# A mixture-of-experts trunk: the first expert position goes from 128 slots and split weights to 64 slots in two column tiles and whole weights

## The chip, the cores and the metric

One NeuronCore of a Trainium2 chip runs the whole program. The metric is the device time of one execution in microseconds, the median of several runs.

## The reference, cut to what matters

A two-layer trunk over 272 tokens (16 meta tokens are dropped at the end) of width 1024, in float32. Each layer has a recurrence, a convolution and an output projection; layer 0 then has a dense SwiGLU, and layer 1 a mixture of eight experts of which each token takes two:

```python
D_MODEL, SEQ, N_EXPERTS, TOP_K, D_FF_EXPERT = 1024, 256, 8, 2, 3584

def moe_swiglu(x, w_router, w_gate, w_up, w_down):
    t = x.reshape(B * L, D)
    logits = (t @ w_router).astype(jnp.float32)
    top_val, top_idx = lax.top_k(logits, TOP_K)
    top_w = jax.nn.softmax(top_val, axis=-1)
    gates = jnp.sum(jax.nn.one_hot(top_idx, N_EXPERTS) * top_w[..., None], axis=1)
    out = jnp.zeros_like(t)
    for e in range(N_EXPERTS):
        out = out + gates[:, e:e + 1] * swiglu(t, w_gate[e], w_up[e], w_down[e])
    return out.reshape(B, L, D)          # swiglu: (silu(x @ w_gate) * (x @ w_up)) @ w_down
```

On the inputs used, the 256 kept tokens fall on the experts 0 to 7 as 179, 20, 32, 107, 98, 10, 2 and 64 (each token counts twice).

## The kernel before

All weights pass once through the core, in pieces of 128 x 1024 float32 (512 KB each, a few of 256 KB). Pieces 0 to 243 (`DENSE`) belong to the two mixers and the dense layer, the last of them to `w_hg_out` (8 pieces) and `w_out` (8). The 672 pieces behind them are the eight experts, 84 for each: 28 gate, 28 up, 28 down. SyncE (SP) issues every load, in one order, from one queue.

The experts are worked off by **position**. Position 0 is always expert 7 (`FIRST`), so that its loads need not wait for the routing; positions 1 to 7 are the other experts by falling number of tokens. The order is 0, 2, 3, 4, 5, 6, 7 (`ORDER`), and the pieces of position 1 (`SIDE`) are strewn among those of 4 to 7. Each position has a number of **slots**, the tokens that it can hold: 128 (`CAP`) for 0, 2 and 3, 192 for 1, 64 (`SLIM`) for 4, 32 (`THIN`) for 5 to 7. Tokens beyond the slots are worked off at the end in `moe_rest`, behind a branch that is taken if the counter `over` is above zero.

- Positions 0, 2 and 3 are **split** (`moe_item`): ScalarE rounds a loaded piece to its high part `whi` (L128), VectorE takes the rest as `wlo` (L106; GpSimd at L347 for two pieces), and TensorE multiplies three times, high by high, high token part by high, high by low (L1575 to L1577 for gate and up, L1569 to L1571 for down). That is 504 matmuls of 512 columns for a position.
- Positions in `LANES` are **plain** (`plain_item`): a piece is multiplied as float32 as it lies, without splits (L1639 gate and up, L1617 down). 64 slots fill half the columns of the array, so two column tiles of 64 work beside each other.

Loaded pieces lie in three pools: `raw` (6 tiles), `wsplit` (tags `whi` and `wlo`, 6 each), and `halves` (17 tiles, tag `hs`). A split piece is loaded to `raw`, and may also go to `hs` while its number is from `AHEAD` (250) to `END` (340): six pieces by turns (`in_hs`). A plain piece may also lie in a free `whi` or `wlo` (`place`). `prep` and `top_up` load as far ahead as tiles are free. A pool `moe` (tag `four`, 6 tiles) is opened when the mixer's memory is given back; two of its tiles hold the rows of a layer norm.

Ahead of position 0, `route` computes each token's slot (`key`), `affine` finishes the layer norm of the token tiles `ht` (tiles named `res`), `gather` splits `ht` into `hp` tiles (`hh`, `hl`) and multiplies them by a one-hot matrix `oh` to collect the tokens of position 0 in `xg`. `warm` issues matmuls on ones (L183). Later gathers are tasks, strewn between items: `G23`, where the gather of positions 2 and 3 begins, is group 4 of position 0's seven.

Of the kernel before, what the change touches and what calls it, by code (L numbers as in the profile page):

```python
# [7 lines left out]
F32 = mybir.dt.float32  # L8
# [34 lines left out]
LANES = {1: ((1, CAP), (SECOND, SLIM)), 4: ((4, SLIM),), 5: ((5, THIN),), 6: ((6, THIN),), 7: ((7, THIN),)}  # L43
# [9 lines left out]
AHEAD, EXTRA, END = DENSE + 6, 6, 340  # L53
# [13 lines left out]
G23, GSL, GW = (0, 4), (2, 3), (3, 1)  # L67
# [63 lines left out]
class Trunk:  # L131
# [101 lines left out]
    def plan(self):  # L233
# [42 lines left out]
        self.units = u + self.moe_units(self.moe_seq([0]))  # L276
        self.plain = set()
# [3 lines left out]
        self.held, self.done = {"raw": [], "whi": [], "wlo": []}, 0  # L281

    def load_ahead(self, upto):
        while len(self.loaded) < min(upto, len(self.units)):
# [3 lines left out]
            if self.in_hs(i):  # L288
                t = self.hs.tile([P, GR], F32, tag="hs", name=self.name("raw"))
            else:  # L290
                where = self.place(i) or "raw"
                t = (self.rawp if where == "raw" else self.wp).tile([P, GR], F32, tag=where, name=self.name("raw"))
                self.held[where].append(i)
# [5 lines left out]
    def place(self, i):  # L299


        for where in ("whi", "wlo") if i in self.plain else ():
            if sum(j >= self.done for j in self.held[where]) + min(self.splits(i), SPLIT - 1) < SPLIT:
                return where
        return "raw" if sum(j >= (self.done if j in self.plain else len(self.ready)) for j in self.held["raw"]) < RAW else None

    def top_up(self):
        while len(self.loaded) < len(self.units) and not self.in_hs(len(self.loaded)) and self.place(len(self.loaded)):
            self.load_ahead(len(self.loaded) + 1)
# [5 lines left out]
    def prep(self, upto, late=None):  # L315


        while len(self.ready) < min(upto, len(self.units)):
            i = len(self.ready)
            if i < END:  # L320
                n, room = i, {False: RAW, True: EXTRA}
                room[self.in_hs(i)] += 1
                while room[self.in_hs(n)]:
                    room[self.in_hs(n)] -= 1
                    n += 1
                self.load_ahead(n)
            else:
                self.top_up()
# [11 lines left out]
            if late is None:  # L340
                step = m // 2 if self.urgent(i) else m
                for a in range(0, m, step):
                    c = slice(a, a + step)
                    self.split(hi[:, c], lo[:, c], t[:, c], eng)
            else:
                self.A.activation(hi[:, :m], t[:, :m], AF.Copy)
                late.append(lambda a=(lo[:, :m], t[:, :m], f32(hi[:, :m])), eng=eng: eng.tensor_tensor(*a, op=ALU.subtract))  # L347
            self.ready.append([a[:, :m].rearrange("p (k n) -> p k n", k=k) for a in (hi, lo)])
        if len(self.ready) >= END:
            self.top_up()  # L350
# [4 lines left out]
    def in_hs(self, i):  # L355
        return AHEAD <= i < END and (i - AHEAD) % (RAW + EXTRA) < EXTRA

    def lo_pool(self, i):
        if i >= DENSE:
            return DENSE + 4 <= i < DENSE + 6  # L360
        return i != 1 and i < 93 or 156 <= i < DENSE - 8

    def take(self, n):

        i = self.used
        self.used += n
# [966 lines left out]
    def overflow(self, count):  # L1333
# [4 lines left out]
        for j, (p, cap) in enumerate(((0, CAP), (1, FULL), (2, CAP), (4, SLIM), (5, THIN))):  # L1338
# [61 lines left out]
    def moe_seq(self, positions, plain=()):  # L1400
# [4 lines left out]
        for p in positions:  # L1405
# [7 lines left out]
            for i, item in enumerate(items):  # L1413
                seq.append(item)
                for _ in range(int(SIDES[p][i]) if p in plain else 0):
                    seq.append(extra.pop(0))
# [51 lines left out]
    def gather(self, ps, key, width, now=False, first=None):  # L1468
# [6 lines left out]
        def tiles():  # L1475
# [5 lines left out]
            if first:  # L1481
                first()
# [30 lines left out]
        else:  # L1513
            self.tasks += todo

# [75 lines left out]
    def plain_item(self, kind, p, g):  # L1591
# [382 lines left out]
```

## Time and profile before

| | |
|---|---|
| median of 3 runs | 1868.27 us (1864.24 to 1871.71) |
| the profiled execution | 1871.86 us, of which the span (first to last instruction) is 1870.1 us |
| TensorE busy | 1783.0 us (95%) |
| VectorE, ScalarE, GpSimd busy | 1062.9 us (57%), 801.4 us (43%), 483.7 us (26%) |
| read from memory | 481.73 MB, 258 GB/s over the span |
| mean granted TensorE clock | 0.980 |

The expert part begins at 933.58 us of the span. A span row gives times from the first instruction; the time of an execution is 1.8 us longer than its span. A busy share says nothing on what bounds a stretch; the waits of that stretch do. PE is TensorE, PEld its weight loads, SPq the load queue on SyncE; a float32 matmul shows as two records.

### The profile page before, as it was taken

The page shows a single profiled execution, that of the slowest core. Times are in us where ns is not written, and L with a number is a line of the kernel's source. Part 1 is how long each engine was busy: PE and PEld are TensorE (multiplying, and loading weights), DVE is VectorE, ACT ScalarE, POOL GpSimd, SP SyncE. Part 2 cuts the span into 40 slices and gives each one's busy share as a digit, 9 for nine tenths or more (in the row PEclk, how much of TensorE's full clock was granted, in tenths as well). Part 3 has the DMA queues.
Part 4 walks back from the last instruction along what each step waited for, and adds up shares of the span by engine and source line. Part 5 has one row for each costly group of instructions (what it writes and reads, how often), then busy time and mean ns, then how long its engine had stood idle before and what let it go on. Part 6 is the DMA issues. An engine that isn't in the chain of part 4 may idle for free. (4 is left out here: it accounts for less than half of the span.)

```text
span 1870.1 us, 31403 instructions
## 1 busy us (share of the span) xinstructions
PE 1783.0 (95%) x11934; PEld 1362.3 (73%) x11934; DVE 1062.9 (57%) x1630; ACT 801.4 (43%) x1211; POOL 483.7 (26%) x258
## 2 busy tenths in 40 slices
PE   9989999899999998999899999999999989999996
PEld 8989899799999998899888888887333323333332
DVE  6999834865556899825799998987000001100104
ACT  5535545454445544555477877776001000000011
POOL 6857656510007856755200000000000000000000
PEclk9999999999999999999999999999999999999998
DMA  6634344455555544335579899999999999999995
GB/s 212 181 107 146 98 125 136 135 172 178 177 161 152 168 123 125 112 114 178 201 293 377 291 340 359 355 342 389 407 401 406 406 398 405 405 400 400 387 404 206
DMA packets 259589, 484.93 MB, mean 259 GB/s; under 512 B 15042, under 2 KB 139842, under 8 KB 259430
## 3 DMA queue, kind: packets, MB, share of 16 engines
q1 hardware_dynamic: 259078, 481.75, 72.1%
q8 instruction: 96, 1.57, 0.3%
q0 software_dynamic: 320, 1.08, 0.1%
q14 instruction: 63, 0.52, 0.1%
q10 hardware_dynamic: 32, 0.01, 0.0%
HBM read 481.73 MB, written 1.05 MB: 258 GB/s over the span
## 5 line engine op out<-in xcount | busy, mean ns | idle before, releaser
L128 ACT ACTIVATE whi<-raw 128x1024 fp32r<-128x1024 f32 (+1 forms) x498 | 519.0, 1050 | 114.4 <-PE mm L1576 42.9
L230 POOL TENSOR_TENSOR wlo<-raw,whi 128x1024 fp32r<-128x1024 f32 (+1 forms) x173 | 418.7, 2439 | 371.6 <-ACT whi L128 358.2
L106 DVE TENSOR_TENSOR wlo<-raw,whi 128x1024 fp32r<-128x1024 f32 (+1 forms) x323 | 386.4, 1218 | 93.3 <-ACT whi L128 82.1
L399 PE MATMUL mm<-h_hi,whi 128*128 128x272 f32 (+1 forms) x1280 | 378.4, 296 | 1.0 <-ACT tmp L128 1.0
L401 PE MATMUL mm<-h_hi,wlo 128*128 128x272 f32 (+1 forms) x1280 | 371.0, 290 | 0.0
L400 PE MATMUL mm<-h_lo,whi 128*128 128x272 f32 (+1 forms) x1280 | 369.8, 289 | 0.0
L1639 PE MATMUL mm<-raw,xg 128*32 128x256 f32 (+4 forms) x2464 | 327.4, 418 | 21.0 <-DMA raw<-in_moe_w_up_dram 17.7
L1639 PEld LDWEIGHTS mm<-raw,xg 128*32 128x32 f32 (+2 forms) x2464 | 116.9, 125 | 230.4 <-issue 143.4
L399 PEld LDWEIGHTS mm<-h_hi,whi 128*128 128x128 f32 x1280 | 244.6, 191 | 2.7 <-ACT tmp L128 1.2
L400 PEld LDWEIGHTS mm<-h_lo,whi 128*128 128x128 f32 x1280 | 244.8, 191 | 0.1
L401 PEld LDWEIGHTS mm<-h_hi,wlo 128*128 128x128 f32 x1280 | 244.2, 191 | 0.0
L1884 POOL TENSOR_TENSOR res<-res,four 128x256 f32<-128x256 f32 x2 | 2.3, 1141 | 931.0 <-ACT res L128 931.0
L106 DVE SCALAR_TENSOR_TENSOR st<-wide,cw,st 128x272 f32<-128x272 f32 (+1 forms) x480 | 194.5, 490 | 0.0
L1575 PE MATMUL mm<-whi,xg 128*128 128x512 f32 x336 | 133.0, 396 | 0.0
L1576 PE MATMUL mm<-whi,xg 128*128 128x512 f32 x336 | 131.7, 392 | 0.0
L1577 PE MATMUL mm<-wlo,xg 128*128 128x512 f32 x336 | 131.5, 391 | 0.0
L1685 DVE TENSOR_TENSOR tmp<-tmp,mm 128x512 f32<-128x512 f32 (+2 forms) x37 | 21.4, 579 | 147.9 <-PE mm L1639 134.1
L128 ACT ACTIVATE tmp<-ca 128x256 f32<-128x256 f32 (+5 forms) x43 | 17.7, 413 | 204.3 <-PE ca L1690 171.7
L1617 PE MATMUL st<-raw,tmp 128*32 128x512 f32 (+1 forms) x448 | 88.7, 599 | 5.7 <-DMA raw<-in_moe_w_down_dram 5.4
L128 ACT ACTIVATE tmp<-mm 128x272 f32<-128x272 f32 (+3 forms) x75 | 33.4, 449 | 123.4 <-PE mm L1639 80.9
L1685 DVE TENSOR_TENSOR four<-four,mm 128x512 f32<-128x512 f32 (+1 forms) x14 | 7.1, 551 | 134.3 <-PE mm L1639 134.3
L1577 PEld LDWEIGHTS mm<-wlo,xg 128*128 128x128 f32 x336 | 63.5, 189 | 13.7
(350 smaller groups left out, 2695.9 us busy)
## 6 DMA issues: line engine op xcount, KB each, us to landing
raw<-in_moe_w_gate_dram SPq DMA_DIRECT2D x224, 512.0 KB, 10.1
raw<-in_moe_w_up_dram SPq DMA_DIRECT2D x224, 512.0 KB, 10.1
raw<-in_moe_w_down_dram SPq DMA_DIRECT2D x224, 512.0 KB, 10.1
raw<-in_w_in_dram SPq DMA_DIRECT2D x128, 512.0 KB, 3.8
raw<-in_ffn_w_gate_dram SPq DMA_DIRECT2D x22, 512.0 KB, 3.6
raw<-in_ffn_w_up_dram SPq DMA_DIRECT2D x22, 512.0 KB, 3.5
raw<-in_ffn_w_down_dram SPq DMA_DIRECT2D x20, 512.0 KB, 3.5
raw<-in_w_conv_out_dram SPq DMA_DIRECT2D x16, 512.0 KB, 3.3
```

The source lines that it names most:

```text
L106: return f(out, *a, **k)
L128: return self.eng.activation(out, in_, func, **k)
L230: (eng or self.V).tensor_tensor(lo, src, f32(hi), op=ALU.subtract)
L399: nc.tensor.matmul(ps[c], w[i][0][:, a], xh, start=first, stop=False)
L400: nc.tensor.matmul(ps[c], w[i][0][:, a], xl, start=False, stop=False)
L401: nc.tensor.matmul(ps[c], w[i][1][:, a], xh, start=False, stop=last)
L1575: nc.tensor.matmul(bank, x[0](k), whi, start=k == 0, stop=False)
L1576: nc.tensor.matmul(bank, x[1](k), whi, start=False, stop=False)
L1577: nc.tensor.matmul(bank, x[0](k), wlo, start=False, stop=k == KB - 1)
L1617: nc.tensor.matmul(y[c][tile[i % m], :], f(i), w[i - h][:, 0, c * 512:(c + 1) * 512], start=begin and i < m, stop=end and i >= n // P - m)
L1639: nc.tensor.matmul(bank[t, :m], self.x[q][0](k), w[:, i, j * m:(j + 1) * m], start=k == 0, stop=k == KB - 1)
L1685: nc.vector.tensor_tensor(f, self.sg.pop(p), bank, op=ALU.mult)
```

## The change

Position 0 joins `LANES` with 64 slots: its weights are not split, its groups are 1024 wide (four instead of seven, `GROUPS`), and its items are done by `plain_item`. Up to 30 of its pieces may lie on chip early: 8 in `hs`, 4 in `four`, 12 in `whi` and `wlo`, 6 in `raw`. Pieces behind these use `whi`, `wlo` and `raw` alone. Its tokens are gathered by `gather_first`, which multiplies the unsplit float32 rows `ht` by `oh`; the split rows `hh` and `hl`, which the later gathers need, are made behind that. `G23` is now group 1 of position 0's four. In `plain_item`, where a piece holds two blocks of k, the lanes are now the outer loop and the blocks the inner one. `overflow` and `moe_rest` count position 0 from 64.

```diff
-LANES = {1: ((1, CAP), (SECOND, SLIM)), 4: ((4, SLIM),), ...}
+LANES = {0: ((0, SLIM),), 1: ((1, CAP), (SECOND, SLIM)), 4: ((4, SLIM),), ...}
...
-AHEAD, EXTRA, END = DENSE + 6, 6, 340
+END, EXTRA = DENSE + 30, {"hs": 8, "four": 4}
...
-G23, GSL, GW = (0, 4), (2, 3), (3, 1)
+G23, GSL, GW = (0, 1), (2, 3), (3, 1)
...
     def place(self, i):
-        for where in ("whi", "wlo") if i in self.plain else ():
-            if sum(j >= self.done for j in self.held[where]) + min(self.splits(i), SPLIT - 1) < SPLIT:
-                return where
-        return "raw" if sum(j >= (self.done if j in self.plain else len(self.ready)) for j in self.held["raw"]) < RAW else None
+        live = {w: sum(j >= (self.done if j in self.plain else len(self.ready)) for j in x) for w, x in self.held.items()}
+        if i in self.plain:
+            for where, n in EXTRA.items():
+                if i < END and live[where] < n and (where == "hs" or self.mp):
+                    return where
+            for where in ("whi", "wlo"):
+                if live[where] + min(self.splits(i), SPLIT - 1) < SPLIT:
+                    return where
+        return "raw" if live["raw"] < RAW else None
...
     def prep(self, upto):
-            if i < END:
-                ...
-                self.load_ahead(n)
-            else:
-                self.top_up()
+            if i < DENSE:
+                self.load_ahead(min(i + RAW + 1, DENSE))
+            if i + RAW >= DENSE:
+                self.top_up()
...
+    def gather_first(self, ht, key):
+        nc = self.nc
+        oh, x = self.one_hot([0], key, SLIM), self.hs.tile([P, KB, SLIM], F32, tag="hs", name=self.name("xg"))
+        self.affine[1]()
+        for kk in range(KB // 2):
+            pt = self.ca((P, 2, SLIM))
+            for i in range(2):
+                k = 2 * kk + i
+                for tt in (1, 0):
+                    nc.tensor.matmul(pt[:, i], ht[tt][:, k * P:(k + 1) * P], f32(oh[:, tt, 0]), start=tt == 1, stop=tt == 0)
+            dst = x[:, 2 * kk:2 * kk + 2]
+            if kk % 2:
+                self.A.activation(dst, pt, AF.Copy)
+            else:
+                nc.vector.tensor_copy(dst, pt)
+        self.x[0] = [lambda k: x[:, k, :], {"left": 0, "oh": oh}, 0]
...
     def plain_item(self, kind, p, g):
-            for i in range(b):
-                k = b * h + i
-                for (q, _, tile), bank in zip(lanes, banks):
-                    m = n // len(tile)
+            for (q, _, tile), bank in zip(lanes, banks):
+                m = n // len(tile)
+                for i in range(b):
+                    k = b * h + i
...
     def moe(self, ht):
-        self.prep(self.used + SPLIT, late)
+        self.prep(self.used + SPLIT)
         key = self.route()
         seq = self.moe_seq(ORDER, LANES)
+        self.gather_first(ht, key)
         hh, hl = [...]
-        self.A.activation(hh[1], ht[1], AF.Copy)
-        ...
-        self.gather([0], key, CAP, True, rest)
+        for tt in (1, 0):
+            self.A.activation(hh[tt], ht[tt], AF.Copy)
+            nc.vector.tensor_tensor(hl[tt], ht[tt], f32(hh[tt]), op=ALU.subtract)
+        self.exps()
```

The load queue on SP, around the middle of the `w_hg_out` pieces, before; `raw` are pieces, and in brackets stand the engines (or the earlier transfers, DMAHW) that an issue waits for:

```order
L296 DMA raw_9461<-in_w_hg_out_dram 128x4x256 [waits DMAHW3_49,Pool_49]
L296 DMA raw_9508<-in_w_hg_out_dram 128x4x256 [waits DMAHW4_49,Pool_49]
L296 DMA raw_9557<-in_w_hg_out_dram 128x4x256 [waits DMAHW5_49,Pool_49]
L296 DMA raw_9598<-in_w_hg_out_dram 128x4x256 [waits DMAHW6_49,Pool_49]
L296 DMA raw_9631<-in_w_hg_out_dram 128x4x256 [waits DMAHW7_49,Pool_49]
L296 DMA raw_9662<-in_w_hg_out_dram 128x4x256 [waits DMAHW0_49,Pool_49]
L296 DMA raw_9695<-in_w_out_dram 128x4x256 [waits DMAHW1_49,Pool_49]
```

The same place in the change:

```order
L297 DMA raw_9461<-in_w_hg_out_dram 128x4x256 [waits DMAHW3_49,Pool_49]
L297 DMA raw_9508<-in_w_hg_out_dram 128x4x256 [waits DMAHW4_49,Pool_49]
L297 DMA four_10167<-in_moe_w_up_dram 128x1024 [waits DVE_49,PE_49]
L297 DMA four_10169<-in_moe_w_up_dram 128x1024
L297 DMA raw_9557<-in_w_hg_out_dram 128x4x256 [waits DMAHW5_49,Pool_49]
L297 DMA four_10171<-in_moe_w_up_dram 128x1024 [waits DMAHW6_49]
L297 DMA raw_9598<-in_w_hg_out_dram 128x4x256 [waits DMAHW7_49,Pool_49]
L297 DMA raw_9631<-in_w_hg_out_dram 128x4x256 [waits DMAHW0_49,Pool_49]
L297 DMA four_10173<-in_moe_w_up_dram 128x1024 [waits DMAHW1_49]
L297 DMA raw_9662<-in_w_hg_out_dram 128x4x256 [waits DMAHW2_49,Pool_49]
```

Four up pieces of position 0, in `four` tiles, now stand between the last `w_hg_out` pieces; the first waits for VectorE and TensorE, the last readers of the mixer's memory.

The load queue behind the last `w_out` pieces, before (`raw_10003` is the last of them, then come the first pieces of position 0):

```order
L296 DMA raw_9963<-in_w_out_dram 128x4x256 [waits DMAHW7_49,DVE_49]
L296 DMA raw_10003<-in_w_out_dram 128x4x256 [waits DMAHW0_49,DVE_49]
L296 DMA raw_10040<-in_moe_w_gate_dram 128x2x512 [waits DMAHW1_49,DVE_49]
L296 DMA raw_10075<-in_moe_w_gate_dram 128x2x512 [waits DMAHW2_49,DVE_49]
L296 DMA raw_10153<-in_moe_w_gate_dram 128x2x512 [waits DMAHW3_49,DVE_49,Activation_49]
L296 DMA raw_10159<-in_moe_w_gate_dram 128x2x512 [waits DMAHW4_49,DVE_49,Activation_49]
L296 DMA raw_10195<-in_moe_w_up_dram 128x2x512 [waits DMAHW5_49,DVE_49]
L296 DMA raw_10201<-in_moe_w_up_dram 128x2x512 [waits DMAHW6_49,DVE_49]
L296 DMA raw_10203<-in_moe_w_up_dram 128x2x512 [waits PE_49]
L296 DMA raw_10205<-in_moe_w_up_dram 128x2x512 [waits PE_49]
```

And in the change:

```order
L297 DMA raw_10003<-in_w_out_dram 128x4x256 [waits DMAHW4_49,DVE_49]
L297 DMA raw_10040<-in_moe_w_gate_dram 128x1024
L297 DMA raw_10042<-in_moe_w_gate_dram 128x1024 [waits PE_49]
L297 DMA raw_10044<-in_moe_w_gate_dram 128x1024 [waits DMAHW5_49,PE_49]
L297 DMA raw_10046<-in_moe_w_gate_dram 128x1024 [waits DMAHW6_49,PE_49]
L297 DMA raw_10048<-in_moe_w_gate_dram 128x1024 [waits DMAHW7_49]
L297 DMA raw_10050<-in_moe_w_gate_dram 128x1024 [waits DMAHW0_49]
L297 DMA raw_10052<-in_moe_w_gate_dram 128x1024 [waits DMAHW1_49]
L297 DMA raw_10054<-in_moe_w_gate_dram 128x1024 [waits DMAHW2_49,PE_49]
L297 DMA raw_10056<-in_moe_w_up_dram 128x1024 [waits DMAHW3_49]
L297 DMA raw_10058<-in_moe_w_up_dram 128x1024 [waits DMAHW4_49]
L297 DMA raw_10093<-in_moe_w_up_dram 128x1024 [waits DMAHW5_49,DVE_49]
```

The first eight gate pieces, in `hs` tiles, wait for no split any more but for TensorE's last reads of the tiles, and the pieces behind them follow as the `w_out` pieces are split or used.

TensorE's queue where position 0 begins, before: behind the warming on ones the gather, whose 32 matmuls read the split rows `hp`:

```order
L183 MATMUL ca_10482<-ones 128x128 x14
L1491 MATMUL ca_10535<-oh_10517,hp_10512 128x128
L1491 MATMUL ca_10535<-oh_10517,hp_10513 128x128
L1491 MATMUL ca_10535<-oh_10517,hp_10512 128x128
L1491 MATMUL ca_10535<-oh_10517,hp_10513 128x128
L1491 MATMUL ca_10541<-oh_10517,hp_10512 128x128
```

And in the change, from the same warming to the first gate pieces:

```order
L183 MATMUL ca_10476<-ones 128x128 x14
L1516 MATMUL ca_10512<-oh_10506,res_9773 128x64
L1516 MATMUL ca_10512<-oh_10506,res_9772 128x64
...
L1516 MATMUL ca_10530<-oh_10506,res_9773 128x64
L1516 MATMUL ca_10530<-oh_10506,res_9772 128x64
L1647 MATMUL mm_10548<-raw_10040,xg_10509 64x512 x2
L1647 MATMUL mm_10548<-raw_10042,xg_10509 64x512 x2
L1647 MATMUL mm_10548<-raw_10044,xg_10509 64x512 x2
```

The gather has 16 matmuls, reads the rows `res` themselves, and the first gate matmuls stand right behind it, two for each piece (one to a column tile).

## Rows read from the trace of the kernel before

**Rows 1.** Page: span, busy time by engine, DMA rate in 40 slices.

```profile
span 1870.1 us, 31403 instructions
...
PE 1783.0 (95%) x11934; PEld 1362.3 (73%) x11934; DVE 1062.9 (57%) x1630; ACT 801.4 (43%) x1211; POOL 483.7 (26%) x258
...
GB/s 212 181 107 146 98 125 136 135 172 178 177 161 152 168 123 125 112 114 178 201 293 377 291 340 359 355 342 389 407 401 406 406 398 405 405 400 400 387 404 206
```

**Rows 2.** Waits of the load queue, before and behind 1306 us: total, times, longest.

```profile
SPq L296 <- DVE wlo L106: 203.9, 200, 9.2
...
SPq L296 <- DMA raw<-in_moe_w_up_dram: 102.0, 137, 1.5
```

**Rows 3.** Windows, us: busy time, instructions, granted clock, DMA share, rate.

```profile
1020.00:1290.00 270.00, 270.00 (x1262) 224.69 (x1261) 248.03 (x241) 213.24 (x233) 0.00 (x0) 1.00 0.95 342
1306.00:1840.00 534.00, 509.30 (x3241) 179.15 (x3240) 52.11 (x87) 39.40 (x85) 0.00 (x0) 0.98 1.03 402
```

**Rows 4.** TensorE in time: first matmuls of positions 0 and 2.

```profile
933.58 0.73 PE L1575 MATMUL mm<-whi,xg 128*128 128x512 f32 x1
...
1057.87 0.39 PE L1571 MATMUL st<-wlo,fs 128*128 128x512 f32 x1
1058.10 0.39 PE L1575 MATMUL mm<-whi,xg 128*128 128x512 f32 x1
```

**Rows 5.** TensorE in time: the first gate and up groups of position 4.

```profile
1306.05 7.09 PE L1639 MATMUL mm<-raw,xg 128*64 128x512 f32 x32
...
1313.44 7.09 PE L1639 MATMUL mm<-raw,xg 128*64 128x512 f32 x32
```

**Rows 6.** TensorE in time: warming and gather ahead of position 0.

```profile
914.67 1.01 PE L1183 MATMUL st<-rw,tmp 128*128 128x8 f32 x8
...
921.79 3.37 PE L183 MATMUL ca<-ones 128*128 128x128 f32 x28
```

**Rows 7.** The load queue in time, from the last w_out piece.

```profile
882.32 0.37 SPq L296 DMA_DIRECT2D raw<-in_w_out_dram  x1
885.77 9.35 SPq L296 DMA_DIRECT2D raw<-in_moe_w_gate_dram  x4
...
904.35 8.58 SPq L296 DMA_DIRECT2D raw<-in_moe_w_up_dram  x4
929.34 3.62 SPq L296 DMA_DIRECT2D raw<-in_moe_w_down_dram  x4
```

**Rows 8.** Windows around the routing, columns as in rows 3.

```profile
920.00:924.00 4.00, 2.76 (x25) 2.79 (x26) 3.83 (x11) 1.69 (x2) 0.41 (x1) 1.00 0.00 0
```

**Rows 9.** Last reader of the mixer's memory, then hg_out loads.

```profile
839.09 0.39 PE L930 MATMUL ca<-att,vt 64*128 64x16 f32 x2
...
840.36 5.07 SPq L296 DMA_DIRECT2D raw<-in_w_hg_out_dram  x2
```

**Rows 10.** Issue to landing of the loads from 826 to 860 us.

```profile
DMA to landing us min/median/max: 3.4/3.8/4.8
```

**Rows 11.** Halves of a split piece, 1058 to 1306 us, by shape.

```profile
L106 DVE TENSOR_TENSOR wlo<-raw,whi 128x1024 fp32r<-128x1024 f32 x164 | 197.5, 1223 | 19.7 <-ACT whi L128 11.2
...
L128 ACT ACTIVATE whi<-raw 128x1024 fp32r<-128x1024 f32 x163 | 172.7, 1062 | 50.8 <-PE mm L1576 27.8 <-PE st L1570 13.3 <-DVE wlo L106 5.2
```

**Rows 12.** TensorE in time, waiting for loads, position 5 or later.

```profile
1510.06 0.64 PE L1639 MATMUL mm<-raw,xg 128*32 128x256 f32 x8 [0.67 <-DMA raw<-in_moe_w_up_dram]
1511.36 1.08 PE L1639 MATMUL mm<-raw,xg 128*32 128x256 f32 x8 [0.67 <-DMA raw<-in_moe_w_up_dram]
1512.80 15.38 PE L1639 MATMUL mm<-raw,xg 128*128 128x512 f32 x48 [0.36 <-DMA raw<-in_moe_w_gate_dram]
```

**Rows 13.** Windows of that stretch, TensorE alone: busy, clock, DMA.

```profile
1506.00:1512.00 6.00, 2.66 (x36) 0.89 1.04 393
1512.00:1518.00 6.00, 5.64 (x18) 0.54 1.04 405
1518.00:1524.00 6.00, 6.00 (x24) 1.00 1.03 405
```

More of the change, by code (lines that the diff above doesn't have):

```diff
@@ L275, in plan @@
         layer(1)
-        self.units = u + self.moe_units(self.moe_seq([0]))
-        self.plain = set()
+        self.units, self.plain = u, set()
+        self.add_units(self.moe_seq([0], LANES), LANES)
         self.loaded = []
@@ L280, in plan @@
         self.used = 0
-        self.held, self.done = {"raw": [], "whi": [], "wlo": []}, 0
+        self.held, self.done = {"raw": [], "whi": [], "wlo": [], "hs": [], "four": []}, 0
     def load_ahead(self, upto):
@@ L287, in load_ahead @@
             src = src() if callable(src) else src
-            if self.in_hs(i):
-                t = self.hs.tile([P, GR], F32, tag="hs", name=self.name("raw"))
-            else:
-                where = self.place(i) or "raw"
-                t = (self.rawp if where == "raw" else self.wp).tile([P, GR], F32, tag=where, name=self.name("raw"))
-                self.held[where].append(i)
+            where = self.place(i) or "raw"
+            self.held[where].append(i)
+            if where == "four":
+                t = self.four(F32)
+            else:
+                pool = {"raw": self.rawp, "hs": self.hs}.get(where, self.wp)
+                t = pool.tile([P, GR], F32, tag=where, name=self.name("raw"))
             k, n = src.shape[1], src.shape[2]
@@ L313, in splits, with prep @@
         return sum(i not in self.plain for i in range(self.done, end)) if self.plain else 0
-    def prep(self, upto, late=None):
+    def prep(self, upto):
         while len(self.ready) < min(upto, len(self.units)):
             i = len(self.ready)
-            if i < END:
[L321 to L325, printed above, removed]
-                self.load_ahead(n)
-            else:
+            if i < DENSE:
+                self.load_ahead(min(i + RAW + 1, DENSE))
+            if i + RAW >= DENSE:
                 self.top_up()
@@ L339, in prep @@
             eng = self.nc.gpsimd if self.lo_pool(i) else self.V
[L340 to L347, printed above, removed]
+            step = m // 2 if self.urgent(i) else m
+            for a in range(0, m, step):
+                c = slice(a, a + step)
+                self.split(hi[:, c], lo[:, c], t[:, c], eng)
             self.ready.append([a[:, :m].rearrange("p (k n) -> p k n", k=k) for a in (hi, lo)])
-        if len(self.ready) >= END:
+        if len(self.ready) >= DENSE:
             self.top_up()
@@ L365, in take @@
         i = self.used
+        self.done = i
         self.used += n
@@ L1337, in overflow @@
         self.over = self.cp.tile([P, 1], I32, name="over")
-        for j, (p, cap) in enumerate(((0, CAP), (1, FULL), (2, CAP), (4, SLIM), (5, THIN))):
+        for j, (p, cap) in enumerate(((0, SLIM), (1, FULL), (2, CAP), (4, SLIM), (5, THIN))):
             v.tensor_scalar(t[:, j:j + 1], count[:, p:p + 1], -float(cap), 0.0, op0=ALU.add, op1=ALU.max)
@@ L1414, in moe_seq @@
                 seq.append(item)
-                for _ in range(int(SIDES[p][i]) if p in plain else 0):
+                for _ in range(int(SIDES[p][i]) if p in SIDES and plain else 0):
                     seq.append(extra.pop(0))
@@ L1466, in gather_slim, with gather @@
         self.tasks += [lambda: box.update(oh=self.one_hot(ps, key, SLIM))] + [slice_(kk) for kk in range(KB // 2)]
-    def gather(self, ps, key, width, now=False, first=None):
+    def gather(self, ps, key, width, now=False):
         nc = self.nc
```

29 lines of the change are left out of this document (5 added, 24 removed).

## The prediction

> **What bounds the kernel now.** I read the page first: TensorE is busy 95% of the span, yet the load rate changes: 100 to 212 GB/s in the first half, 290 to 390 from about 980 us, about 400 from 1310 us on [rows 1]. So the share of busy time hides stages, and the expert part (from 933.58 us, [rows 4]) has two. The waits of the load queue tell them apart [rows 2]: up to 1306 us it waits for `wlo` on VectorE, that is, for a tile that a split gives back; behind 1306 us it waits for earlier transfers. The windows agree [rows 3]: from 1020 to 1290 us TensorE has no idle time and loads run at 342 GB/s; from 1306 to 1840 us loads run at 402 GB/s, and TensorE has 25 us idle. So the split positions 0, 2, 3 are bound by TensorE (VectorE, 248 of 270 us, is close behind), and the plain positions 4 to 7 with 1 strewn in are bound by loads: 512 KB at 402 GB/s is 1.30 us for a piece.
>
> Position 0 takes 1058.10 - 933.58 = 124.5 us [rows 4], 1.48 us for each of 84 pieces. Positions 2 and 3 take 1306.05 - 1058.10 = 248 us [rows 4, 5]. From there to the end of the span are 564 us [rows 1, 5].
>
> **The change part by part.**
>
> *Plain weights in two column tiles.* All 84 splits of position 0 go: 1.06 us on ScalarE and 1.22 us on VectorE each [rows 11], of which nothing was on the path, since TensorE had no idle time. What counts is TensorE's own time. Position 4 already works with 64 slots: 32 records, eight pieces, take 7.09 us [rows 5], 0.89 us for a piece. 84 pieces take 74.8 us. Before, position 0 spent its 124.5 us on 504 matmuls of 0.23 us (the pitch of the starts at 1057.87 and 1058.10, [rows 4]), 116 us, and some 8.5 us on a slow start, transposes and the gather of 2 and 3. At most these 8.5 us stay. TensorE alone would need 75 to 83 us.
>
> *The gather.* Before, the first matmul of position 0 ran at 933.58 us at a lowered clock (0.73 us). Now 16 float32 matmuls follow the warming, which ends at 921.79 + 3.37 = 925.2 us; 32 records at 0.12 us (eight float32 records of 8 columns in 1.01 us) are 3.9 us, and records of 128 columns cost the same (28 of the warming in 3.37 us) [rows 6]. The rows of `res` are ready by then, since the `hp` tiles that the old gather read are made from them. I take 929.0 us as the start: 4.5 us early, bounds 0 and 5. Making `hh` and `hl` moves behind it, beside position 0, where VectorE has no splits; without that cover it would cost its 3 us.
>
> *Early loads.* Before, 16 pieces were issued by 912.9 us and the next at 929.34 [rows 7], with no byte moving from 920 to 924 us [rows 8]. Now 30 are. Four stand between `w_hg_out` loads and wait for the mixer's last reader, a matmul at 839.09 us; the next `w_hg_out` load left at 840.36 and the one behind it at 845 [rows 9], so nothing queued behind them is late for that, and 4 x 1.30 us of transfer falls into slices of 114 to 178 GB/s [rows 1]. Cost: nothing, at most 5 us if the split that needs the delayed piece had no lead. The others follow the last `w_out` piece (882.32 us): 26 x 1.30 = 34 us, 916 us, the last held back by reads of the last `w_out` pieces until about 913 us, as before [rows 7], so landed by 920 us, 9 us before use.
>
> *What the loads then do to position 0.* The first eight pieces lie in `hs` and pieces 12 to 15 in `four`; these free nothing for the expert queue. So piece 31 is issued when piece 9 is done: 929.0 + 9 x 0.89 = 937.0 us, and the queue is idle for 17 us. Piece 34 waits for piece 16: 943.2 us. A load lands 3.8 us behind its issue when the queue is short [rows 10], so piece 34 lands at 947.0 us; from there the queue stays full, and piece 84 lands at 947.0 + 50 x 1.30 = 1012 us. TensorE, at 0.89 us a piece or 0.99 with all of the other work, catches up with the loads somewhere from piece 64 to the last; I take 74, and from there it waits for each. Both limits end close to each other: TensorE alone 1004 to 1012 us, loads 1012 us.
>
> *Position 2.* Its first pieces may lie in `raw` alone, and six of them are issued while position 0 uses its last 16. The first lands at 1013.4 us, is split in 1.06 + 1.22 us [rows 11], and TensorE begins position 2 at 1015.7 us instead of 1058.1: **42.4 us early**. Its next pieces come every 1.30 us, it needs one every 1.48 us; I take off 1.4 us for unevenness. The bound there is 12 x 1.30 = 15.6 us: before, the first twelve pieces of position 2 could also lie in `hs`, now they cannot.
>
> *Loop order in `plain_item`, loads of `over`, larger program.* The loop order touches only position 1's gate and up pieces, in the stage that waits for loads: nothing, with 25 us of idle time [rows 3] as cover; from a gain of 0 to a loss of 5.
>
> *Sum.* 42.4 - 1.4 = 41 us; positions 2 and 3 keep their 248 us and the stage behind them its 564. The profiled execution was 1871.9 us, so 1830.9 us by it; it lies 3.6 us above the median of the runs, so the forecast for a median is 1868.3 - 41 = **1827 us**.
>
> **A rule on the clock.** Where TensorE waited for every piece (busy 2.66 of 6 us) its clock was granted at 0.89 and then 0.54, about the lower level of 1.2 GHz, and eight matmuls of the same kind went from 0.64 to 1.08 us; the window behind shows 1.00 again [rows 12, 13]. In position 0 TensorE would wait for pieces 74 to 84 with 0.89 us of work in 1.30, so its waits are shorter than its work, while in [rows 12] the wait is 0.67 us for 0.64 of work. I take no loss. The Trainium skill, page "TensorE: Matmul & The Clock Gate", section "HAM oscillation — how this bites in real kernels", says that bursts of matmuls with longer waits for data between them drop to the low clock and pay for it burst by burst. It speaks against putting TensorE behind loads; the rows bear it out where waits are as long as the work, and show nothing for waits half as long. By the rule the sum would be the one of the second rival.
>
> **The rivals.**
>
> 1. *The split stage starts cold.* Position 2 begins without stock, and TensorE waits for loads and splits. For it: VectorE is at 92% in that stage [rows 3]. Against: 1.30 us of load and 1.22 us of VectorE are both below 1.48. Price up to 15.6 us: 1842 us.
> 2. *The clock falls at the end of position 0.* Eleven pieces at 2 x 0.89 = 1.77 us instead of 1.30 are 5 to 6 us: 1833 us.
> 3. *The change doesn't load early.* If only 16 pieces were there at 929 us, 68 would follow: 929.0 + 3.8 + 68 x 1.30 = 1021 us instead of 1012, 9 us less gain: 1836 us. Against it stands the order of the queue.
> 4. *Nothing gained.* If loads bound the whole expert part, TensorE's saving would be hidden. Against: 342 against 402 GB/s [rows 3]. 1868 us.
> 5. *Slower: overflow.* With 65 tokens in position 0, `over` is above zero and `moe_rest` does the expert again in split form: 124.5 us and 11 us of gather and first loads, 1963 us. The reference's routing gives it exactly 64; the nearest outsider misses it by 0.004 in its logit. Decided at the 65th token.
>
> **How the numbers follow.** Forecast 0.70, rivals 1 to 5: 0.12, 0.07, 0.05, 0.03, 0.03. The forecast's own range is 1817 to 1837: start 929 to 934, load price 1.28 to 1.34, loss on position 2's first pieces 0 to 5, and 3 us between runs. The 8-in-10 range takes in rivals 1 to 3: 1814 to 1845. Under 0.5% (9 us, about what a measurement here can tell) fall rival 4 (same 0.03) and above it rival 5 (slower 0.03); the rest is faster, 0.94.
>
> **What would show it.** In the changed kernel's profile: first gate matmul near 929 us; no loads from about 920 to 937 us; eight plain pieces in 7.1 us; TensorE waiting for loads only in the last dozen pieces of position 0; first split matmul near 1016 us, first plain matmul of position 4 near 1264 us, and 564 us from there. I am wrong if the load rate in position 0 stays under 380 GB/s behind 947 us, if positions 2 and 3 take more than 252 us, if the clock is under 0.9 between 990 and 1016 us, or if matmuls of `moe_rest` appear.

## The result, and the profile after

The changed kernel takes **1837.88 us** (median of 4 runs, 1833.08 to 1837.99); the kernel before, on the same chip, 1869.99 us (1864.24 to 1873.23). The ratio is 0.9827, with a 95% interval of 0.9807 to 0.9847: 32 us faster. The forecast was 1827 us, the range 1814 to 1845. The profiled execution took 1837.85 us, its span is 1836.1 us.

The page after: span, busy times, clock and rate in 40 slices, beside [rows 1].

```profile
span 1836.1 us, 30767 instructions
...
PE 1739.6 (95%) x11784; PEld 1302.5 (71%) x11784; DVE 954.4 (52%) x1537; ACT 712.4 (39%) x1120; POOL 476.9 (26%) x255
...
GB/s 216 174 114 139 103 127 130 146 161 173 167 178 135 182 132 116 126 112 210 322 200 403 369 363 354 359 349 393 406 402 405 407 398 403 404 398 400 387 403 195
```

TensorE's share is 95% as before, so the page shows no gain in it: the same share is reached on less work, 1739.6 us instead of 1783.0. The new row of rates shows where: one slice falls to 200 GB/s (918 to 964 us) and the next is at 403, where the slices of before had 293 (935 to 982 us) and 377 (982 to 1029 us). The time is best laid out by stages, each from one first matmul to the next, in us:

| | before | after | forecast |
|---|---|---|---|
| position 0 begins | 933.58 | 931.70 | 929.0 |
| position 0 lasts | 124.5 | 87.0 | 86.7 |
| positions 2 and 3 last | 247.95 | 251.85 | 249.4 |
| from position 4 to the end | 564.05 | 565.5 | 564.05 |
| span | 1870.1 | 1836.1 | 1829.1 |

Against before: -1.9 - 37.5 + 3.9 + 1.5 = -34.0 us. TensorE in time after, ahead of position 0 and in its first groups (beside [rows 4, 6]), then position 4 (beside [rows 5]):

```profile
922.70 0.24 PE L1284 MATMUL ca<-sel,count_before 128*128 128x8 f32 x1 [2.97 <-DVE sel L1282]
...
923.25 5.00 PE L183 MATMUL ca<-ones 128*128 128x128 f32 x28
928.09 3.68 PE L1516 MATMUL ca<-oh,res 128*128 128x64 f32 x32
931.70 9.66 PE L1647 MATMUL mm<-raw,xg 128*64 128x512 f32 x44
...
953.04 7.09 PE L1647 MATMUL mm<-raw,xg 128*64 128x512 f32 x32
...
1270.58 7.09 PE L1647 MATMUL mm<-raw,xg 128*64 128x512 f32 x32
```

Eight plain pieces take 7.09 us, as forecast, and the gather 3.68 us. But the 28 records of warming ahead of it take 5.00 us and not the 3.37 of [rows 6]. The windows (TensorE alone: busy, clock, DMA share, rate) show why in the first two of these rows, and what the loads do in the others:

```profile
924.00:926.00 2.00, 2.00 (x12) 0.52 0.00 0
926.00:928.00 2.00, 2.00 (x14) 0.63 0.00 0
...
930.00:940.00 10.00, 10.00 (x56) 1.00 0.01 2
940.00:950.00 10.00, 10.00 (x50) 1.00 0.76 256
950.00:960.00 10.00, 10.00 (x48) 1.00 1.01 396
...
1000.00:1010.00 10.00, 9.62 (x45) 1.00 1.02 408
1010.00:1020.00 10.00, 8.74 (x33) 1.00 1.04 395
```

The granted clock is 0.52 and 0.63, about the lower level of 1.2 GHz, behind 2.97 us in which TensorE waited for `sel`. In these rows loads stand still from 924 to 940 us, and from 950 us on they run at about 400 GB/s. The load queue in time after, beside [rows 7, 9]; the four `four` pieces left among the `w_hg_out` loads (the first two are shown), the thirtieth piece at 915.03 us, and the next at 939.69:

```profile
842.36 0.93 SPq L297 DMA_DIRECT2D four<-in_moe_w_up_dram  x2
...
896.25 11.18 SPq L297 DMA_DIRECT2D raw<-in_moe_w_gate_dram  x8
907.48 7.50 SPq L297 DMA_DIRECT2D raw<-in_moe_w_up_dram  x5
915.03 1.60 SPq L297 DMA_DIRECT2D raw<-in_moe_w_up_dram  x1
939.69 0.33 SPq L297 DMA_DIRECT2D raw<-in_moe_w_up_dram  x1
941.40 9.77 SPq L297 DMA_DIRECT2D raw<-in_moe_w_down_dram  x8
```

TensorE in time in the last groups of position 0 and in the first pieces of position 2:

```profile
992.47 4.08 PE L1647 MATMUL mm<-raw,xg 128*64 128x256 f32 x32
...
999.51 1.08 PE L1647 MATMUL mm<-raw,xg 128*64 128x256 f32 x8 [0.28 <-DMA raw<-in_moe_w_up_dram]
1000.87 1.08 PE L1647 MATMUL mm<-raw,xg 128*64 128x256 f32 x8 [0.27 <-DMA raw<-in_moe_w_up_dram]
...
1013.64 4.56 PE L1625 MATMUL st<-raw,tmp 128*64 128x512 f32 x16
1018.73 0.50 PE L1583 MATMUL mm<-whi,xg 128*128 128x512 f32 x1 [0.53 <-ACT whi L128]
...
1019.99 0.50 PE L1585 MATMUL mm<-wlo,xg 128*128 128x512 f32 x1 [0.53 <-DVE wlo L106]
...
1028.18 0.41 PE L1732 MATMUL ca<-ident,tmp 128*128 128x128 f32 x2 [2.75 <-DVE tmp L1723]
```

The last row is a wait that the kernel before did not have: the transposes of position 0's one-hot matrix. Because the matrix now has 64 slots, `turned` copies it on VectorE first (L1723), and that copy stands behind splits and the rounding of position 0's output. VectorE in time there:

```profile
1022.80 3.84 DVE L106 TENSOR_TENSOR wlo<-raw,whi 128x1024 fp32r<-128x1024 f32 x3 [0.21 <-ACT whi L128]
1026.56 1.28 DVE L106 TENSOR_TENSOR four<-st,four 128x512 fp32r<-128x512 f32 x2
1027.76 0.28 DVE L1723 COPY tmp<-oh 128x256 f32<-128x256 f32 x1
```

From position 4 on nothing is new (beside [rows 3], 402 GB/s with TensorE 31 us idle):

```profile
1272.00:1806.00 534.00, 502.75 (x3238) 189.71 (x3234) 51.34 (x86) 38.73 (x83) 0.00 (x0) 0.97 1.03 402
```

### The profile page after: what moved, and what is told of

Its sections match the earlier page's. It is cut to its first block, busy times and chain, and to the rows that moved or that the text cites. A ratio compares the mean times of both kernels' runs of the same rounds, so it can differ in the third digit from the quotient of the medians.

```text
span 1836.1 us, 30767 instructions
## 1 busy us (share of the span) xinstructions
PE 1739.6 (95%) x11784; PEld 1302.5 (71%) x11784; DVE 954.4 (52%) x1537; ACT 712.4 (39%) x1120; POOL 476.9 (26%) x255
## 3 DMA queue, kind: packets, MB, share of 16 engines
q0 software_dynamic: 320, 1.08, 0.2%
## 5 line engine op out<-in xcount | busy, mean ns | idle before, releaser
L128 ACT ACTIVATE whi<-raw 128x1024 fp32r<-128x1024 f32 (+1 forms) x414 | 430.6, 1048 | 102.7 <-PE mm L1584 18.4
L1647 PE MATMUL mm<-raw,xg 128*32 128x256 f32 (+4 forms) x2704 | 361.3, 430 | 25.6 <-DMA raw<-in_moe_w_up_dram 21.2
L106 DVE TENSOR_TENSOR wlo<-raw,whi 128x1024 fp32r<-128x1024 f32 (+1 forms) x241 | 288.0, 1215 | 95.7 <-ACT whi L128 88.8
L1647 PEld LDWEIGHTS mm<-raw,xg 128*32 128x32 f32 (+2 forms) x2704 | 143.0, 127 | 238.8 <-issue 134.2
L1625 PE MATMUL st<-raw,tmp 128*32 128x512 f32 (+1 forms) x560 | 123.4, 599 | 7.3 <-DMA raw<-in_moe_w_down_dram 6.0
L1625 PEld LDWEIGHTS st<-raw,tmp 128*32 128x32 f32 (+1 forms) x560 | 31.0, 120 | 84.8 <-issue 40.6
L128 ACT ACTIVATE tmp<-mm 128x272 f32<-128x272 f32 (+2 forms) x72 | 31.5, 441 | 149.3 <-PE mm L1647 106.8
L1583 PE MATMUL mm<-whi,xg 128*128 128x512 f32 x224 | 88.2, 394 | 0.5 <-ACT whi L128 0.5
L1585 PE MATMUL mm<-wlo,xg 128*128 128x512 f32 x224 | 87.5, 391 | 0.5 <-DVE wlo L106 0.5
L1584 PE MATMUL mm<-whi,xg 128*128 128x512 f32 x224 | 87.3, 390 | 0.0
```

Source lines behind the costliest of these rows:

```text
L106: return f(out, *a, **k)
L128: return self.eng.activation(out, in_, func, **k)
L1583: nc.tensor.matmul(bank, x[0](k), whi, start=k == 0, stop=False)
L1584: nc.tensor.matmul(bank, x[1](k), whi, start=False, stop=False)
L1585: nc.tensor.matmul(bank, x[0](k), wlo, start=False, stop=k == KB - 1)
L1625: nc.tensor.matmul(y[c][tile[i % m], :], f(i), w[i - h][:, 0, c * 512:(c + 1) * 512], start=begin and i < m, stop=end and i >= n // P - m)
```

## The experiments

The theory behind them: the gain is TensorE's own time in position 0, which comes from the two column tiles; early pieces are worth only as much as the loads trail TensorE at the end of position 0. The rival: the early loads are the gain, and each is worth its 1.30 us. All kernels below are edits of the changed kernel. Their stages, read at the same three matmuls as in the table above, in us; "count" is the time from the first counting matmul (L1284) to the first gate matmul, which leaves out the up to 4 us by which executions already differ before this place (counting begins between 919.0 and 922.9 us). The kernel before measured 1867.89 us beside the first four experiments and 1870.56 us, on another chip, beside the last four; the ratios take this difference in, the medians do not:

| | count | position 0 | positions 2, 3 | from 4 | median (low to high) | ratio to before (95%) |
|---|---|---|---|---|---|---|
| before | 12.3 | 124.5 | 247.95 | 564.05 | | |
| after | 9.0 | 87.0 | 251.85 | 565.5 | 1837.88 (1833.08 to 1837.99) | 0.9807 to 0.9847 |
| no early tiles | 7.4 | 93.05 | 253.6 | 565.35 | 1842.67 (1841.29 to 1844.47) | 0.9842 to 0.9880 |
| tiles reused | 9.0 | 80.9 | 249.8 | 565.15 | 1828.72 (1825.45 to 1830.24) | 0.9767 to 0.9802 |
| one-hot early | 9.0 | 87.9 | 250.5 | 564.8 | 1835.09 (1828.84 to 1839.44) | 0.9792 to 0.9838 |
| warming moved | 5.8 | 86.75 | 252.0 | 565.3 | 1834.12 (1830.40 to 1837.53) | 0.9796 to 0.9835 |
| split gather | 12.0 | 87.7 | 253.7 | 564.5 | 1841.61 (1839.74 to 1843.83) | 0.9830 to 0.9857 |
| old loop order | 9.0 | 87.1 | 253.6 | 566.2 | 1837.04 (1835.97 to 1841.12) | 0.9813 to 0.9842 |
| 128 slots | 9.0 | 150.7 | 248.4 | 564.15 | 1894.41 (1892.55 to 1895.20) | 1.0109 to 1.0140 |
| three edits | 5.8 | 81.1 | 249.85 | 565.6 | 1825.65 (1816.89 to 1827.01) | 0.9721 to 0.9764 |

**No early tiles.**

```diff
-END, EXTRA = DENSE + 30, {"hs": 8, "four": 4}
+END, EXTRA = DENSE + 30, {}
```

> The change without its early tiles in hs and four: at most 18 pieces of position 0 (12 in whi and wlo, 6 in raw) are there when it begins, and tiles come back from its first piece on. My theory (the saving is TensorE's own time, and early pieces are worth only what the loads trail at the end of position 0): piece 19 is issued at 931.7 + 0.9 = 932.6 us and lands at 936.4, the other 65 follow at 1.30 us and the last lands at 1021 us, so position 0 takes 90 to 92 us instead of 87.0, position 2 starts 3 to 5 us later, and the time is 1841 to 1843 us. Rival (the early pieces are the gain, each saves its load of 1.30 us): 12 x 1.30 = 15.6 us are lost, 1853 us. Second rival (TensorE alone bounds position 0): 0, 1838 us.

Measured: 1842.67 us, 4.8 us more than the change (the intervals of the ratios overlap a little). Position 0 takes 93.05 us, 1 us above the theory's 90 to 92, and position 2 begins at 1021.69 us. The rival's 15.6 us did not come. TensorE in time, whose first wait for a load in position 0 comes 27 us earlier than in the change:

```profile
972.50 1.08 PE L1647 MATMUL mm<-raw,xg 128*64 128x512 f32 x4 [0.21 <-DMA raw<-in_moe_w_gate_dram]
...
1021.69 0.50 PE L1583 MATMUL mm<-whi,xg 128*128 128x512 f32 x1 [0.55 <-ACT whi L128]
```

So twelve early pieces are worth about 5 us here (6.0 in position 0 itself), not 15.6: without them, tiles come back from the first piece on and the queue starts again earlier (329 GB/s from 930 to 940 us, where the change has 2). The two other stages nearly cancel: the clock held in the warming (count 1.6 us shorter) and fell to 0.5 from 1033 to 1036 us instead (positions 2 and 3 take 1.7 us longer).

**Tiles reused through position 0.**

```diff
-END, EXTRA = DENSE + 30, {"hs": 8, "four": 4}
+END, EXTRA = DENSE + 84, {"hs": 8, "four": 4}
```

> The change with END = DENSE + 84: the tiles of hs and four are used again through all of position 0, so the load queue begins again with the first piece done, at 932.6 us, instead of about 937 to 941 us, and ends earlier. My theory (TensorE bounds nearly all of position 0, since it waits for loads for under 1 us in its last 20 us, and what the earlier loads give is only a stock for position 2): position 0 takes 85 to 87 us, and the time is 1834 to 1838 us. Rival (the idle 17 us of the load queue are the bound of position 0): 13 pieces x 1.30 us earlier, position 0 takes 75 to 80 us and the time is 1823 to 1828 us. Second rival (the tiles of hs then are in the way of what positions 2 and 3 keep there): slower, above 1842 us.

Measured: 1828.72 us, 9.2 us less than the change. My theory failed here: position 0 takes 80.9 us, 4 to 6 us less than its 85 to 87, and the time is 5 us below its range. The rival was nearer, as it put the bound on the idle load queue; it missed its 75 to 80 us and its 1823 to 1828 us by about 1 us. TensorE has no wait left in position 0 of this kernel, so TensorE's own time is now the limit there. Windows and queue of this kernel:

```profile
920.00:930.00 10.00, 7.80 (x56) 0.83 0.55 219
930.00:940.00 10.00, 10.00 (x54) 1.00 0.58 210
...
1000.00:1010.00 10.00, 10.00 (x50) 1.00 0.68 239
```

```profile
906.98 8.93 SPq L297 DMA_DIRECT2D raw<-in_moe_w_up_dram  x8
915.95 24.42 SPq L297 DMA_DIRECT2D raw<-in_moe_w_down_dram  x8
```

The gap of the queue is partly filled even before TensorE begins position 0 (at 931.20 us): two of the down pieces leave by 918.1 us, so 34 pieces are out and not 30. These four did not wait for any piece of position 0; by the kernel, `hs` has 17 tiles, and a piece that takes the next of them need not wait for the piece that frees its place in the count. The other six down pieces leave from 932.32 us on, where the change begins again at 939.69. Then TensorE no longer meets the loads:

```profile
1003.01 0.59 PE L1625 MATMUL st<-four,tmp 128*64 128x512 f32 x1
1003.02 0.59 PE L1625 MATMUL st<-raw,tmp 128*64 128x512 f32 x1
1003.44 0.59 PE L1625 MATMUL st<-four,tmp 128*64 128x512 f32 x1
1003.45 0.59 PE L1625 MATMUL st<-raw,tmp 128*64 128x512 f32 x1
...
1008.50 3.65 PE L1625 MATMUL st<-raw,tmp 128*64 128x512 f32 x16
1012.09 0.50 PE L1583 MATMUL mm<-whi,xg 128*128 128x512 f32 x1
...
1019.48 0.41 PE L1732 MATMUL ca<-ident,tmp 128*128 128x128 f32 x2 [1.62 <-DVE tmp L1723]
```

The last 16 records of position 0 take 3.65 us here and took 4.56 in the change. There lies my error: I read the cost of late loads from the waits that stand in brackets, which add up to 0.8 us. The starts of single records show what these leave out. In the down pieces one column tile works on one piece and the other tile on the next, so the records go in pairs, as in the first four rows: both start within 0.01 us, and the next pair follows after 0.43 us. In the change, four of the last 16 records stand alone (at 1015.41, 1015.84, 1017.18 and 1017.61 us), so there are ten such steps instead of eight. One tile went on by itself there while the other had nothing to do, and the profile counts TensorE as busy. That the other tile's piece had not landed yet is my reading, since with the loads ahead of TensorE the same records go in pairs. With the stock position 2 also starts without its two waits for `whi` and `wlo`.

**One-hot turned early.** The transposes become a task at the start of group 2 of position 0.

```diff
+                           (0, 2): lambda: self.turn_ahead(0),
                            (7, 1): lambda: self.spread_rows("ln2_g", "ln2_b"),
```

> The change, and the transposed one-hot of position 0 is made by a task at the start of group 2 of position 0 and not when position 2 has begun. My theory (the 2.75 us that TensorE waits at 1028.18 us come from a VectorE copy of the one-hot that stands behind splits, and are most of what position 2 and 3 take more than before): the wait goes, positions 2 and 3 take 249 us instead of 251.9, and the time is 1835 us. Rival (TensorE is ahead of splits there, and without this wait it waits for the next wlo): the stage stays at 251 to 252 us and the time at 1838 us.

Measured: 1835.09 us; its interval overlaps that of the change, so the time alone decides nothing. The stage does. The task waits its turn behind those of the gather, so the transposes run just ahead of position 2, at 1017.98 us. The wait at L1732 is gone, but 1.1 us of it come back one step later, for ScalarE's copy of the transposed matrix (at 1026.01 us), which stands behind its rounding of position 0's output:

```profile
1017.98 0.44 PE L1732 MATMUL ca<-ident,tmp 128*128 128x128 f32 x2
...
1026.45 1.12 PE L1770 MATMUL ca<-four,four 128*128 128x512 f32 x2 [1.09 <-ACT four L128]
```

Positions 2 and 3 take 250.5 us instead of 251.85, and position 0, which now holds the transposes, 0.9 more: a net gain of about 0.5 us in these stages, nearer to the rival. The 2.75 us wait was real, yet it covered others.

**Warming moved ahead of the routing result.** Twelve matmuls more ahead of it, seven fewer behind it.

```diff
-WARM = 22, 4, 11, 14, 13
+WARM = 22, 4, 23, 7, 13
```

> The change with another split of the warming matmuls ahead of position 0: 23 instead of 11 in the third group and 7 instead of 14 in the fourth, the one ahead of the gather. My theory (the gather began at 928.09 us though its inputs were there at 925.34, because the 14 warming matmuls ran at a granted clock of 0.52 to 0.63 after an idle of 2.97 us): the gather begins 2 us earlier, position 0 at 929 to 930 us, and the time is 1836 us. Rival (the low clock then falls on the gather and the first gate matmuls, which cost what the warming no longer does): position 0 begins at 929 to 930 us but its first eight pieces take more than 9 us, and the time stays at 1838 us.

Measured: 1834.12 us, 3.8 us less than the change, intervals overlapping. TensorE in time:

```profile
922.50 0.24 PE L1284 MATMUL ca<-sel,count_before 128*128 128x8 f32 x1 [0.31 <-DVE sel L1282]
...
923.05 1.81 PE L183 MATMUL ca<-ones 128*128 128x128 f32 x14
924.69 3.68 PE L1516 MATMUL ca<-oh,res 128*128 128x64 f32 x32
928.31 9.66 PE L1647 MATMUL mm<-raw,xg 128*64 128x512 f32 x44
```

From counting to the first gate matmul are 5.8 us instead of 9.0, more than the theory's 2: half of it is the low clock, half the 14 records that no longer stand ahead of the gather. The rival fails: the gather and the first eleven pieces take 3.68 and 9.66 us, as in the change.

**Gather from split rows**, on top of the moved warming.

```diff
-                for tt in (1, 0):
-                    nc.tensor.matmul(pt[:, i], ht[tt][:, k * P:(k + 1) * P], f32(oh[:, tt, 0]), start=tt == 1, stop=tt == 0)
+                for tt in (1, 0):
+                    for part in range(2):
+                        nc.tensor.matmul(pt[:, i], self.parts[part][tt][:, k * P:(k + 1) * P], oh[:, tt, 0],
+                                         start=tt > part, stop=tt < part)
...
-        self.affine[1]()
...
-        self.gather_first(ht, key)
         hh, hl = [...]
+        self.affine[1]()
...
+        self.parts = hh, hl
+        self.gather_first(ht, key)
         self.exps()
-        self.parts = hh, hl
```

> The version with moved warming (1834 us, position 0 from 928.3 us), but position 0 is gathered from the split rows as before: hh and hl are made first, and 32 matmuls read them. My theory (plain rows let the gather begin as soon as key and affine are done; the split rows are there only after two ScalarE roundings and two VectorE differences): TensorE waits 3 to 4 us for the last hp, position 0 begins at 931.5 to 932.5 us, and the time is 1837 to 1839 us. Rival (the split rows are made beside the warming and cost nothing): position 0 begins at 928 to 929 us and the time stays at 1834 us.

Measured: 1841.61 us, 7.5 us above the kernel with moved warming, where 3 to 5 were expected (about 5 by the two ratios, 8 by the stages of the two profiles). The gather in time, and the clock behind its wait:

```profile
927.87 7.01 PE L1516 MATMUL ca<-oh,hp 128*128 128x64 f32 x32 [2.71 <-DVE oh L1420]
```

```profile
930.00:934.00 4.00, 4.00 (x20) 0.50 0.00 0
```

The wait is 2.71 us, a little under the theory's 3 to 4; `oh` is late because it stands on VectorE behind the two differences that make `hl`, which the gather needs as well. The 32 records then take 7.01 us instead of 3.68, at a granted clock of 0.50, and position 0 begins at 934.81 us, where 931.5 to 932.5 was expected. So the plain rows are worth the wait and, here, the low clock behind it.

**Old loop order.**

```diff
-            for (q, _, tile), bank in zip(lanes, banks):
-                m = n // len(tile)
-                for i in range(b):
-                    k = b * h + i
+            for i in range(b):
+                k = b * h + i
+                for (q, _, tile), bank in zip(lanes, banks):
+                    m = n // len(tile)
```

> The change with the old order of loops in plain_item: blocks outer, lanes inner. It touches pieces that hold two blocks of k. My theory (it falls into the stage from position 4 on, which is bound by loads with TensorE idle for 31 of 534 us, and into the last four gate and up pieces of position 0, where there is one lane): nothing, the stage from position 4 takes 565.5 us within 1 us and the time is 1838 us. Rival (lanes that alternate on the two banks cost TensorE, so that it falls behind loads): the stage takes 570 us, the time 1842 us.

Measured: 1837.04 us, the same as the change; the stage from position 4 takes 566.2 us, as the theory has it. In this execution TensorE's clock fell twice, once in the warming and once behind the wait for the transposes, which fits the 253.6 us of its positions 2 and 3. The window behind the second wait:

```profile
1026.00:1030.00 4.00, 4.00 (x12) 0.57 0.94 323
```

**128 slots, plain weights, no column tiles.** Position 0 has `CAP` slots in `LANES`, in its gather, in `overflow` and in `moe_rest`, and groups of 512.

```diff
-LANES = {0: ((0, SLIM),), 1: ((1, CAP), (SECOND, SLIM)), ...}
+LANES = {0: ((0, CAP),), 1: ((1, CAP), (SECOND, SLIM)), ...}
...
-        return GROUPS if plain and p != SIDE else [(c, 512) for c in range(0, FFE, 512)]
+        return GROUPS if plain and p not in (0, SIDE) else [(c, 512) for c in range(0, FFE, 512)]
```

> The change with 128 slots for position 0: its weights stay plain, but its tokens fill all columns of the array, so there are no two column tiles; its groups are 512 wide as before the change. My theory (column tiles make the gain; a plain piece at full width is two float32 matmuls of 512 columns with two records of 0.43 us each, 1.7 us, against 0.89 us in two tiles and 1.48 us split): position 0 takes 84 x 1.7 = 143 us and 6 to 8 us of other work, about 150 us, and the time is 1895 to 1905 us, slower than the kernel before. Rival (not splitting is the gain, whatever the width): position 0 takes at most 115 us, the time at most 1866 us.

Measured: 1894.41 us, slower than before by 1.1 to 1.4%, and half a microsecond below the theory's range. Position 0 takes 150.7 us; the theory said about 150. Its first matmuls, and the transposes in position 2:

```profile
929.82 15.62 PE L1647 MATMUL mm<-raw,xg 128*128 128x512 f32 x36
...
1086.38 0.38 PE L1732 MATMUL ca<-ident,oh 128*128 128x128 f32 x2
```

The first row is 0.434 us for each record, where the two tiles have 7.09 / 32 = 0.222. A record by itself is not quicker with 64 slots: at full width the next record starts after 0.43 us, and with reused tiles the next pair does. So the gain is that two records run beside each other. Leaving out the splits by itself costs 26 us (150.7 against 124.5); 64 slots in two column tiles, together with the wider groups, bring 64 (87.0 against 150.7); no run parts tiles and groups. In the second row the transposes read `oh` itself, without the copy on VectorE and without a wait.

**Three edits together**: tiles reused, one-hot early, warming moved.

> Three edits together: hs and four reused through position 0 (alone 1829 us), the moved warming (alone 1834), the one-hot turned early (alone 1835). My theory (they act at three places: the end of position 0, its start, the beginning of position 2): position 0 begins at 928 us and takes 81 to 82 us with the task, positions 2 and 3 take 248 to 249 us and the rest 565, so the span is 1823 to 1825 us and the time 1825 us. Rival (the earlier start of position 0 finds fewer pieces there, and the waits for loads return at its end): the time is that of the reuse alone, 1828 to 1829 us.

Measured: 1825.65 us, ratio 0.9721 to 0.9764: faster than both kernels, 12 us below the change. The stages lie within 1 us of the theory's (5.8 us from counting, 81.1, 249.85, 565.6), and the granted clock is 1.00 from 920 to 1259 us. TensorE's waits in it from 925 to 1276 us, total, times and longest:

```profile
PE ca L1770 <- ACT four L128: 1.4, 1, 1.4
PE ca L1698 <- DVE tmp L1693: 0.2, 1, 0.2
```

That it is faster than the reuse alone (1828.72 us) is likely but not sure: the ranges of the two overlap, while the intervals of their ratios (0.9721 to 0.9764 and 0.9767 to 0.9802) do not.

## Why the prediction was right, and where its numbers were off

The sign and the mechanism held: TensorE's time in position 0 was the price, and two column tiles cut it. The forecast lies 11 us below the measured median. Of these, 7.0 us are in the stages (1836.1 against 1829.1 of span) and the rest in the base: I took 3.6 us off for a profiled execution above its median; after the change the profiled execution lies on its median, and with a fourth run the median of before is 1869.99.

- **Plain weights in two column tiles.** Right: 0.89 us for a piece, and 80.9 us for TensorE alone where the loads keep up (tiles reused), inside the 75 to 83 of the text. The kernel with 128 slots and the pairs of records show that the tiles do it, not the missing splits.
- **The gather.** The mechanism was right, the size was not: a start at 929.0 us was forecast, 931.70 came. Of the 2.7 us, 1.5 are this execution's later arrival at counting (922.70 us; 921.24 before), and 1.6 are the warming at the low clock, which I had priced at the duration of [rows 6], while the gather itself took 0.3 less. Where the clock held (no early tiles), counting to gate took 7.4 us; the forecast had 7.8. Low clock was in the kernel before too, but from 930 to 938 us, in the end of the gather and position 0's first matmuls.
- **Early loads.** Right: thirty pieces, no bytes from 930 to 940 us, and nothing lost among the `w_hg_out` loads that the trace shows. The experiment without early tiles gives their worth, about 5 us.
- **What the loads then do to position 0.** 87.0 us against 86.7, but TensorE met the loads earlier than at piece 74: its rows slow down from about 991 us on (the one at 992.47 us takes 4.08 us, with reused tiles 3.67), where 20 pieces of position 0 are still to come. That is piece 64, the early end of what the text allowed. Piece 31 left at 939.69 us, behind the 937.0 of the text by just the later start; the first piece of position 2 landed at 1017.62 us (the start of its first `whi`) instead of 1013.4, so the loads lost another 1.5 us on the way. That 87.0 came so near 86.7 is in part luck: the forecast let position 2 begin 2.28 us behind that landing, with both halves of the piece made, and it began 1.11 us behind it, as its first matmul reads `whi` alone. The experiment with reused tiles puts 6 us of the 87.0 on the loads. "TensorE alone 1004 to 1012 us, loads 1012 us" was right that the loads are the later limit, but they came some 6 us behind TensorE's own.
- **Position 2.** The term that was most off beside the start: 1.4 us were taken off for unevenness, 3.9 came. The unevenness itself is there as two waits of 0.53 us for the first `whi` (it falls into position 0's time) and `wlo`. What I had not seen is the copy of the 64-wide one-hot on VectorE, 2.75 us of wait at 1028.18 us; the kernel with 128 slots, which needs no copy, has no such wait, and its stage takes 248.4 us. The 251.85 us lie just under the 252 that the text named as a sign of being wrong. Turning the matrix early brought the stage back by 1.3 us only, because a wait for ScalarE took its place.
- **Loop order, larger program.** Nothing, as forecast; the stage from position 4 lies between 564.05 and 566.2 us in all ten profiles, so its 1.5 us are within what executions differ by.
- **A rule on the clock.** The second rival did not come: with waits of 0.27 us before 1.08 us of work the granted clock stayed at 1.00 from 990 us to the end of position 0. The page "TensorE: Matmul & The Clock Gate" of the Trainium skill (section "HAM oscillation — how this bites in real kernels") speaks of long waits between bursts; for waits of a quarter of the work the rows here show no such loss. The low clock came instead behind a single wait of 2.97 us, in the warming, which none of the rivals had.
- **Other rivals.** The first (the split stage starts cold) came to about 2 us of its 15.6: with a stock (tiles reused) positions 2 and 3 take 249.8 us instead of 251.85. The third, fourth and fifth did not happen; no matmul of `moe_rest` runs.

## What to carry to other kernels

When few enough tokens fit half of the array's columns, compare unsplit float32 in two column tiles with the split form by the measured time of a position over its pieces (here 80.9 / 84 = 0.96 us where loads keep up, against 1.48 split and 150.7 / 84 = 1.79 unsplit at full width), since leaving out the splits alone can lose. When a stage gets faster than its loads, look at what gives tiles back: twelve early tiles brought 5 us, but using them again 9 more. And read waits for loads from the pace of equal groups of records in two kernels, not only from the idle time in the waits: where one of two column tiles waits, TensorE still counts as busy.

## What was not expected of the hardware

Nine of the ten profiles have a wait of TensorE of 2.7 to 3.4 us between 914 us and the first transposes of position 2, and eight of them show a granted clock of 0.50 (1.2 GHz) behind one of these waits, for some 3 us in most, 7 us in the kernel before and 10 us in the split gather, at different places: in the end of the gather and position 0's first matmuls (before), in the warming, where it cost 1.6 us (after, tiles reused, one-hot early, old loop order, 128 slots), in the gather, where it cost 3.3, and on into the first gate matmuls (split gather), or among the first split matmuls of position 2 (no early tiles, and a second time in old loop order and split gather). In the kernel with moved warming the wait of 2.84 us before the transposes was followed by none, nor was the one of 2.75 us in the change. What decides between these places is open. In the version with all three edits, which has no wait above 1.5 us there, the clock stayed at 1.00 from 920 to 1259 us.
